# Two accumulator buffers of 1024 bytes, and a ring of weight buffers that starts 1856 bytes later

## The chip, the cores and the metric

The kernel runs on one core of one Trainium2 chip. The metric is device time in microseconds for one execution; a set of runs is told by its median, lowest and highest.

## The reference

Two transformer blocks run one after the other over 256 tokens of width 2048, in float32. What matters here is that nearly everything is a product of the 256 tokens with a large weight matrix, and that six plus three vectors of modulation come from a single row `c`:

```python
mod = (c_act @ w_ada[l] + b_ada[l])[:, None, :]
sh_a, sc_a, gt_a, sh_f, sc_f, gt_f = jnp.split(mod, N_ADA, axis=-1)
h = rms_norm(x, g_attn[l]) * (1.0 + sc_a) + sh_a
y = parallel_mixers(h, w_in[l], ...)                  # projections, two attentions, output products
x = x + gt_a * y
h = rms_norm(x, g_ffn[l]) * (1.0 + sc_f) + sh_f
x = x + gt_f * conv_ffn(h, w_up[l], w_conv[l], b_conv[l], w_down[l])
```

The second block has the same frame (three vectors from `w_mod`, a pool mixer with `pool_w_in`, `pool_w_grp` and `pool_w_out`), and a last norm.

## The kernel before, in words

**Weights.** Each weight matrix comes from memory in units of two K tiles by 512 columns, 512 KB each. `load_split` (lines 270 to 282) takes a buffer of the ring `raw` (`raw_tile`, line 118: six buffers of 4096 bytes on each partition), loads the unit into it from SyncE's queue, and splits it (lines 156 to 158) into a high part, which ScalarE casts, and a low part, which VectorE subtracts. Both parts lie in one buffer of the ring `hl` (line 279: five buffers of 8192 bytes). With `big=True` (lines 275 and 276) they lie instead in two buffers of the general pool `s4` (28 buffers of 4096 bytes, line 47). That is done for the last units of three products alone: three units at the end of `w_o` (line 992), three at the end of `w_down` (line 1098), five at the end of `pool_w_out` (line 1206).

**Products.** `gemm_gen` (line 366) makes a product in float32r with three passes (high by high, low by high, high by low). A unit gives 12 matmuls on line 378: for each of two token tiles and two K tiles, three of 512 columns. The stationary operand is a tile of activations, always in an `s4` buffer (`hT`, `hN`, `gThi`, `gTlo`, `pair`, `zT` and so on); the operand that streams through is the weight part `hl`. As a rule the six matmuls of one token tile are followed by the six of the other. With `tail` the last units make all matmuls of token tile 0 first and those of token tile 1 afterwards; with `head` the first three units do (lines 384 to 391).

**Modulation.** It is computed on VectorE while the products run. A vector unit (`vec_unit`, line 170) loads 512 KB of `w_ada` or `w_mod` into a buffer of the same ring `raw`, multiplies it with silu(c), which stands in two `s4` buffers, and leaves one sum for each partition in a column of the tile `vs`. `job_vec` (line 177) makes that tile (line 185) for a group of output tiles, adds its two halves at the end (line 189) and hands them on. There are 18 such tiles, all with the tag `vs`, which has two buffers. `pump` issues vector units between the units of a product, at a rate that each product names.

**Order.** Each engine's queue runs in program order. The first stage is scheduled by hand, the rest by the framework, which also places the buffers: a pool's tags in the order of their first use, one buffer behind the other, each as large as the largest tile that it holds.

**Places.** In the built program of before, the small constants come first. The `s4` buffers start at byte 34880 of a partition, 4096 bytes apart, so each starts 2112 bytes past a multiple of 4096. Behind them, at 149568, are the two `vs` buffers (96 bytes each), then the six of `raw` from 149760, the five of `hl` from 174336 and the four of `t2` from 215296. Every buffer of `raw` and `hl` starts 2304 bytes past a multiple of 4096.

Of the kernel before, what the change touches and what calls it, by code (L numbers as in the profile page):

```python
# [9 lines left out]
F32 = mybir.dt.float32  # L10
# [19 lines left out]
def block_pair_kernel(ctx: ExitStack, tc: tile.TileContext, T: dict, out: bass.AP):  # L30
# [54 lines left out]
    def load_c(name):  # L85
        """the row on one partition"""
        cr = [s4([128, 1024], name="crow") for _ in range(2)]
        for h in range(2):
            nc.sync.dma_start(cr[h][0:1, :], T[name][0:1, h * 1024:(h + 1) * 1024])
        return cr  # L90

    def bcast_c(cr, ps):
        """silu of the row, on every partition: [128, 2048], and the four steps that end it"""
        cb = [s4([128, 1024], name="cB") for _ in range(2)]
        acts = []

        def act(h, q, p):
            SC.activation(cb[h][:, q * 512:(q + 1) * 512], p, AF.Silu)
        for h in range(2):
            for q in range(2):  # L100
                p = ps([128, 512], name="cb")
                PE.matmul(p, lhsT=ones[0:1, :], rhs=cr[h][0:1, q * 512:(q + 1) * 512], start=True, stop=True)
                acts.append(lambda h=h, q=q, p=p: act(h, q, p))
                if ps is ps_at:
                    acts.pop()()
        return cb, acts

    def warm(dep, n):
        """products that nobody reads: they keep the array's clock up while it waits"""
        p = ps_at([128, 512], name="warm")  # L110
        for _ in range(n):
            PE.matmul(p[:, :128], lhsT=ones, rhs=dep, start=True, stop=True)

    def pump_to(n):
        """leaves n vector units waiting"""
        pump(max(0, len(jobs) - n))
# [53 lines left out]
    def vec_unit(W, ct, h, cv, acc):  # L170
        """acc <- the part of output tile ct of silu(c) @ W over the half h of K"""
        raw = raw_tile()
        nc.sync.dma_start(raw, T[W][ct, h])
        with tc.issue_after(gate[0]) if gate[0] is not None else nullcontext():
            V.scalar_tensor_tensor(raw, raw, 1.0, cact[cv][h], op0=OP.mult, op1=OP.mult, accum_out=acc)  # L175

    def job_vec(W, cv, cts, fin):
        """fin(columns) of silu(c) @ W for the output tiles cts"""
        n = len(cts)
        st = {}  # L180

        def unit(i, h):
            if i == 0 and h == 0:
                n_s4[0] += 1
                st["vs"] = sp.tile([128, 2, n], F32, name=f"vs_{n_s4[0]}", tag="vs", bufs=2)
            vs = st["vs"]
            vec_unit(W, cts[i], h, cv, vs[:, h, i:i + 1])
            if i == n - 1 and h == 1:
                tt(vs[:, 0], vs[:, 0], vs[:, 1], OP.add)
                fin(vs[:, 0])  # L190
        for i in range(n):
            for h in range(2):
                jobs.append(lambda i=i, h=h: unit(i, h))

    def job_row(W, cv, ct0, bcol, rows):
        """rows[h] = (silu(c) @ W + b)[ct0 * 128 + 1024 h ...] on every partition"""
        for h in range(2):
            def fin(v, h=h):
                tt(v, v, col(bcol + h * 8, 8), OP.add)
                rows[h] = s4([128, 1024], name="row")  # L200
                for q in range(2):
                    p = ps_at([128, 4, 128], name="rb")
                    for i in range(4):
                        j = q * 4 + i
                        PE.transpose(p[:, i, :], v[:, j:j + 1].to_broadcast([128, 128]), ident)
                    SC.copy(rows[h][:, q * 512:(q + 1) * 512], p.rearrange("p a b -> p (a b)"))
            job_vec(W, cv, range(ct0 + h * 8, ct0 + h * 8 + 8), fin)
# [26 lines left out]
    def norm_pair(o, j, sl, xT, rB, A, SH):  # L234
        """o <- split(xT * A * rB + SH) for K tiles 2j, 2j+1 and the tokens sl"""
        n = sl.stop - sl.start
        h = t2([128, 2, 256], name="hn")
        for i in range(2):
            k = 2 * j + i
            V.scalar_tensor_tensor(h[:, i, :n], xT[k // 4][:, k % 4, sl], A[:, k:k + 1], rB[:, sl], op0=OP.mult,  # L240
                                   op1=OP.mult)
            SC.activation(o[:, 0, i, sl], h[:, i, :n], AF.Identity, bias=SH[:, k:k + 1])  # L242
            r = V.scalar_tensor_tensor(o[:, 1, i, sl], h[:, i, :n], SH[:, k:k + 1], o[:, 0, i, sl], op0=OP.add,
                                       op1=OP.subtract)
# [7 lines left out]
    def h_prep(dst, src2, kk, A, SH):  # L252
        """dst <- split(src2 * A + SH) for K tiles kk, kk+1; src2 [128, 2, 256]"""
# [16 lines left out]
    def load_split(blk, n, big=False):  # L270
        """one unit: [128, KT * n], KT K tiles of n columns -> high and low parts [128, KT, n]"""
# [78 lines left out]
    def fill(n):  # L350
        """emits n units of the waiting products"""
        fcredit[0] += n
        while fcredit[0] >= 1.0 and fillers:
            try:
                next(fillers[0])
                fcredit[0] -= 1.0
            except StopIteration:
                fillers.popleft()

    def fill_to(gen):  # L360
        """emits the waiting products up to and with gen"""
# [4 lines left out]
    def gemm_gen(st, W, k0, nk, evac, rate=0.0, tail=0, head=0, kw=None, n=512, pre=(), ps=None,  # L366
                 part=(True, True)):
        """psum[t] = h[t] @ W over nk K tiles; W: units of KT K tiles; k0: first K tile of h, kw of W;
        part: whether this is the first, the last part of the sums in psum"""
# [38 lines left out]
    # the sums of these two chunks stay in psum  # L408
# [27 lines left out]
    for g in range(NG):  # L436
# [9 lines left out]
        if g == 0:  # L446
            # tables for the rotary embeddings
# [34 lines left out]
            def folded(o, n, f0, name):  # L482
                """tables with the gain folded in: g1 cos, g2 sin, g2 cos, g1 sin"""
# [8 lines left out]
    def rope(x1, x2, tabs, H, n):  # L492
        """x1, x2 [128, 2, H, n]; tabs: four [128, 2, n]"""
# [13 lines left out]
    # last K group: everything but the gates first  # L507
# [5 lines left out]
    def job_mod(W, cv, ct_sh, ct_sc, h, SH, A, bsh, bsc, gain):  # L513
        """the half h of SH and of A = (1 + scale) * gain"""
# [100 lines left out]
    # latent norms  # L615
# [7 lines left out]
    # sums of squares for qa, ka  # L623
# [47 lines left out]
    # k, q of attention A  # L671
# [36 lines left out]
    def softmax(ps, P, H, ns, scl):  # L708
        """P[:, h, :ns] = softmax of scl[h] * ps[:, h, :ns]"""
# [51 lines left out]
    def tanh_of(i):  # L761
        """sigmoid(g) = (1 + tanh(g / 2)) / 2; the last factor is in the split of the merged values"""
# [43 lines left out]
    for j in range(4):  # L806
# [3 lines left out]
        # keys: scale by their norm; rotary part shared by the heads  # L810
# [70 lines left out]
    def to_pairs(src, dst):  # L881
        """transposes four K tiles of src[:, t, :], halves and splits them, appends two pair tiles"""
# [31 lines left out]
    def residual_norm(c, t, p, rows, ss, xT):  # L914
        """the residual, its sum of squares and its transpose"""
# [9 lines left out]
    def pre_mean(ss, name):  # L925
        """the part of mean + eps that the first three chunks bring; also fetches the table of the root"""
# [7 lines left out]
    def rsqrt_last(ss, pre, t, name):  # L934
        """1/rms of the tokens of tile t, with one Newton step"""
# [10 lines left out]
    def norm_rows(ss, pre, name):  # L946
        """1/rms of each token, along the free axis of every partition, one token tile at a time"""
# [8 lines left out]
    def norm_pairs(o, js, sl, xT, rB, A, SH):  # L956
        """the same for the pairs js of one chunk, more of it on the scalar engine; overwrites xT"""
# [94 lines left out]
    # the first pairs in two halves of K, while the rest of the modulation arrives  # L1052
# [20 lines left out]
    def settle(c):  # L1073
        """the gated sum so far, onto x"""
# [171 lines left out]
def _layout(x):  # L1246
    """the inputs, rearranged (and repeated nowhere): no arithmetic, no change of type"""
    import numpy as np

    def blocks(w, n):  # L1250
        """[K, N] -> [N / n, K / 256, 128, 2 * n]: units of two K tiles by n columns"""
# [3 lines left out]
    def rows(w):  # L1255
        """[2048, N] -> [N / 128, 2, 128, 1024]: output features on the partitions"""
# [49 lines left out]
```

## Time and profile before

| | before |
|---|---|
| median of three runs | 1757.48 us (1755.73 to 1758.36) |
| the profiled execution: span from its first to its last instruction | 1753.6 us |
| TensorE matmul (PE) busy | 1719.4 us, 98% of the span, 7786 matmuls |
| TensorE weight load (PEld) busy | 1380.1 us, 79% |
| VectorE (DVE) busy | 1374.4 us, 78% |
| ScalarE (ACT) busy | 913.0 us, 52% |
| DMA queue of the weights | 454.19 MB, 77.0% of 16 engines' span |

The three times are of whole executions, the span is that of the one that was profiled; its own time is not listed apart from the three. Busy time of PE is the union of its matmuls' spans. Matmuls overlap in the pipeline, so that one that lasts about 0.39 us can follow the one before after much less. The distance from the start of one to the start of the next, here called the pitch, is what a stream of matmuls costs; it is read from the timeline: a run of n matmuls that lasts T, the last of them as long as the mean, has the pitch (T - mean) / (n - 1).

### The profile page before, as it was taken

The numbers are of one execution on the slowest core, as the hardware profiler recorded it, in microseconds if no ns is written. First come the engines' busy times: TensorE is split into PE (matmuls) and PEld (weight loads), VectorE is DVE, ScalarE is ACT, GpSimd is POOL, SyncE is SP. The second block draws the span as 40 slices with busy tenths as digits, with TensorE's granted clock in tenths as the row PEclk, the third lists the DMA queues.
The fourth block names the chain that finished last, engine by engine and source line by source line (L and its number), as shares of the span: only waits on it lengthen the run. The fifth ranks groups of instructions, "written<-read, shape, count | busy, mean of one in ns | idle before, by whom it ended". The sixth has DMA issues, their size and how long they took to land.

```text
span 1753.6 us, 22010 instructions
## 1 busy us (share of the span) xinstructions
PE 1719.4 (98%) x7786; PEld 1380.1 (79%) x7786; DVE 1374.4 (78%) x2079; ACT 913.0 (52%) x1283; POOL 4.2 (0%) x15
## 2 busy tenths in 40 slices
PE   8899999999999999999999999999999999999997
PEld 6688888878878878888887788777877777887886
DVE  8899899998978768589677676777877878765764
ACT  4644354767854456455455543555345574444443
POOL 0000000000000000000000000000000000000000
PEclk9999999999999999999999999999999999999999
DMA  8999988588879868677877777777877758778752
GB/s 326 338 327 317 330 309 286 192 285 292 284 225 319 285 206 315 213 240 228 297 243 247 232 253 273 251 252 266 269 259 258 252 167 267 261 241 269 237 190 90
DMA packets 127495, 455.59 MB, mean 260 GB/s; under 512 B 14357, under 2 KB 15893, under 8 KB 127385
## 3 DMA queue, kind: packets, MB, share of 16 engines
q1 hardware_dynamic: 127384, 454.19, 77.0%
q8 instruction: 61, 1.00, 0.2%
q14 instruction: 50, 0.40, 0.1%
HBM read 452.04 MB, written 2.10 MB: 259 GB/s over the span
## 4 chain that ended last, share of the span: by engine, by line
PE 88%; DVE 5%; DMA 4%; ACT 2%; issue 1%; ACTq 0%; SPq 0%; DVEq 0%
PE mm L378 79%; PE keep L378 2%; DVE hl L79 2%; DVE raw L175 1%; DMA raw<-in_w_mod 1%; PE tp L1025 1%; DMA raw<-in_w_ada 1%; PE mm L1171 1%; ACT hl L157 1%; PE dots L588 1%; DMA raw<-in_w_up 1%; DMA raw<-in_w_pb 0%; DVE xsq L79 0%; PE tp L1138 0%; DMA raw<-in_pool_w_in 0%
## 5 line engine op out<-in xcount | busy, mean ns | idle before, releaser
L157 ACT CAST hl<-raw 128x1024 fp32r<-128x1024 f32 (+2 forms) x564 | 588.2, 1046 | 639.6 <-PE mm L378 483.1
L79 DVE TENSOR_TENSOR hl<-raw,hl 128x1024 fp32r<-128x1024 f32 (+2 forms) x564 | 679.0, 1215 | 165.1 <-ACT hl L157 163.5
L378 PE MATMUL mm<-hl,hN 128*128 128x512 f32 x2880 | 689.0, 398 | 4.4 <-ACT hN L242 2.4
L378 PEld LDWEIGHTS mm<-hl,hN 128*128 128x128 f32 x2880 | 537.6, 188 | 134.5 <-DVE hN L79 3.4
L175 DVE SCALAR_TENSOR_TENSOR raw<-raw,cB 128x1024 f32<-128x1024 f32 x288 | 351.1, 1222 | 161.4 <-DMA raw<-in_w_mod 127.9
L378 PE MATMUL mm<-hl,hT 128*128 128x512 f32 (+1 forms) x1248 | 297.8, 397 | 7.3 <-ACT hl L157 3.2
L378 PEld LDWEIGHTS mm<-hl,hT 128*128 128x128 f32 x1248 | 234.6, 190 | 62.2 <-ACT hl L157 4.1
L378 PE MATMUL mm<-hl,gThi 128*128 128x512 f32 x704 | 221.1, 396 | 0.2
L378 PEld LDWEIGHTS mm<-hl,gThi 128*128 128x128 f32 x704 | 131.3, 187 | 32.8 <-DVE hl L79 0.8
L378 PE MATMUL mm<-hl,gTlo 128*128 128x512 f32 x352 | 138.2, 396 | 0.0
L378 PE MATMUL mm<-hl,pair 128*128 128x512 f32 x384 | 91.6, 395 | 0.0
L378 PE MATMUL mm<-hl,zT 128*128 128x512 f32 x384 | 89.6, 394 | 0.0
L378 PEld LDWEIGHTS mm<-hl,zT 128*128 128x128 f32 x384 | 71.7, 187 | 17.2
L378 PEld LDWEIGHTS mm<-hl,pair 128*128 128x128 f32 x384 | 71.3, 187 | 16.8
L378 PEld LDWEIGHTS mm<-hl,gTlo 128*128 128x128 f32 x352 | 66.0, 187 | 15.6
L79 DVE TENSOR_TENSOR pacc<-pacc,mm 128x512 f32<-128x512 f32 (+1 forms) x78 | 52.7, 676 | 11.4 <-PE mm L378 10.7
L1029 ACT ACTIVATE cv<-tp,wcv 128x256 f32<-128x256 f32 x88 | 44.9, 562 | 16.0 <-DVE cv L1033 8.5
L378 PE MATMUL mm<-hl,oaT 128*128 128x512 f32 x192 | 48.6, 403 | 0.0
L378 PE MATMUL mm<-hl,obT 128*128 128x512 f32 x192 | 48.0, 400 | 0.0
L378 PE MATMUL keep<-hl,hT 128*128 128x512 f32 x192 | 46.4, 397 | 1.0 <-DVE hl L79 1.0
L378 PEld LDWEIGHTS keep<-hl,hT 128*128 128x128 f32 x192 | 35.8, 188 | 10.1 <-DVE hl L79 2.1
L378 PEld LDWEIGHTS mm<-hl,obT 128*128 128x128 f32 x192 | 35.0, 188 | 8.3 <-DVE obT L79 0.4
(331 smaller groups left out, 1194.7 us busy)
## 6 DMA issues: line engine op xcount, KB each, us to landing
raw<-in_w_ada SPq DMA_DIRECT2D x192, 512.0 KB, 4.7
raw<-in_w_up SPq DMA_DIRECT2D x176, 512.0 KB, 4.6
raw<-in_w_in SPq DMA_DIRECT2D x112, 512.0 KB, 5.2
raw<-in_w_mod SPq DMA_DIRECT2D x96, 512.0 KB, 4.4
raw<-in_w_down SPq DMA_DIRECT2D x88, 512.0 KB, 4.6
raw<-in_pool_w_in SPq DMA_DIRECT2D x64, 512.0 KB, 4.4
raw<-in_w_o SPq DMA_DIRECT2D x32, 512.0 KB, 4.7
raw<-in_pool_w_out SPq DMA_DIRECT2D x32, 512.0 KB, 4.1
```

The lines of the kernel that those rows point to most:

```text
L79: return V.tensor_tensor(o, a, b, op=op)
L157: SC.copy(hi, src)
L175: V.scalar_tensor_tensor(raw, raw, 1.0, cact[cv][h], op0=OP.mult, op1=OP.mult, accum_out=acc)
L378: PE.matmul(ps[t][:, :n], lhsT=st(k0 + k, t, a), rhs=hl[b][:, i, :], start=(part[0] and k == 0 and x == 0), stop=(part[1] and k == nk - 1 ...
L588: PE.matmul(p[:, i, :], lhsT=qiT[h // 8][:, (h % 8) // 2, t * 128:(t + 1) * 128], rhs=kiT[:, h % 2, :ns], start=True, stop=True)
L1025: PE.transpose(p[:, i, t * 128:(t + 1) * 128], u[:, t, f * 128:(f + 1) * 128], ident)
L1029: SC.activation(cv[:, f, :], p[:, i, :], AF.Identity, bias=wcv[:, 3, fi:fi + 1], scale=wcv[:, 2, fi:fi + 1])
L1171: PE.matmul(pv[:, q, :], lhsT=hls[k // 2][wa][:, k % 2, f * 128:(f + 1) * 128], rhs=pooled[i][xb][:, k, :], start=(k == 0 and x == 0), sto ...
```

## The change

The two `vs` buffers get a fixed size of 2 by 128 float32 (1024 bytes) and each tile uses the first n columns of each half:

```diff
             if i == 0 and h == 0:
                 n_s4[0] += 1
-                st["vs"] = sp.tile([128, 2, n], F32, name=f"vs_{n_s4[0]}", tag="vs", bufs=2)
+                st["vs"] = sp.tile([128, 2, 128], F32, name=f"vs_{n_s4[0]}", tag="vs", bufs=2)[:, :, :n]
             vs = st["vs"]
```

The other lines of the diff take comments and docstrings out and leave empty lines in their place, so the line numbers stay. No instruction is added or taken away. Everything that the pool places behind `vs` moves: `raw`, `hl`, `t2` and the small buffers start 2 x 1024 - 2 x 96 = 1856 bytes later. `raw` then starts at 151616 and `hl` at 176192, 64 bytes past a multiple of 4096, with the same steps of 4096 and 8192 bytes as before. The constants and `s4` stay where they are.

## Rows read from the trace of the kernel before

**Rows 1.** The page: busy time of TensorE, and the chain by engine.
```profile
PE 1719.4 (98%) x7786; PEld 1380.1 (79%) x7786; DVE 1374.4 (78%) x2079; ACT 913.0 (52%) x1283; POOL 4.2 (0%) x15
...
PE 88%; DVE 5%; DMA 4%; ACT 2%; issue 1%; ACTq 0%; SPq 0%; DVEq 0%
```

**Rows 2.** Stretches, line 378's matmuls alone: start:end, length, busy (count), clock, DMA, GB/s.
```profile
31.00:96.00 65.00, 59.36 (x245) 0.97 0.92 327
96.00:270.00 174.00, 173.81 (x759) 1.00 0.91 322
270.00:521.00 251.00, 199.79 (x826) 1.00 0.77 260
521.00:613.00 92.00, 88.78 (x374) 1.00 0.87 295
613.00:657.00 44.00, 38.51 (x155) 0.96 0.64 211
657.00:1402.00 745.00, 727.65 (x3067) 1.00 0.77 256
1402.00:1486.00 84.00, 73.60 (x299) 0.98 0.66 214
1486.00:1622.00 136.00, 128.57 (x542) 1.00 0.79 258
1622.00:1720.00 98.00, 71.15 (x305) 1.00 0.65 210
1720.00:1753.60 33.60, 23.97 (x105) 0.92 0.18 63
```

**Rows 3.** Waits, whole span: who waited for whom, us, times, longest.
```profile
ACT hl L157 <- PE mm L378: 483.1, 313, 3.4
...
ACT hl L157 <- DMA raw<-in_w_in: 81.8, 48, 4.0
```

**Rows 4.** Waits, stretch 96 to 270 us.
```profile
ACT hl L157 <- DMA raw<-in_w_in: 70.0, 40, 4.0
ACT hl L157 <- PE mm L378: 18.3, 13, 2.4
```

**Rows 5.** Timeline of TensorE, weights in the ring `hl`: start, us, instruction, count.
```profile
96.31 63.86 PE L378 MATMUL mm<-hl,hT 128*128 128x512 f32 x273
...
1689.82 28.39 PE L378 MATMUL mm<-hl,zT 128*128 128x512 f32 x121
```

**Rows 6.** Timeline of TensorE, ends of `w_o` and `pool_w_out`, weights in `s4`.
```profile
640.46 5.83 PE L378 MATMUL mm<-hl,pair 128*128 128x512 f32 x25
...
1731.34 12.40 PE L378 MATMUL mm<-hl,zT 128*128 128x512 f32 x54
```

**Rows 7.** Timeline of TensorE, first three units of `pool_w_in` (`head`), weights in the ring.
```profile
1434.78 9.49 PE L378 MATMUL mm<-hl,hN 128*128 128x512 f32 x40
```

**Rows 8.** Timeline of the other engines beside the first of rows 6.
```profile
641.25 1.22 DVE L79 TENSOR_TENSOR hl<-raw,hl 128x1024 fp32r<-128x1024 f32 x1 [2.68 <-ACT hl L157]
...
643.15 1.05 ACT L157 CAST hl<-raw 128x1024 fp32r<-128x1024 f32 x1 [1.93 <-DMA raw<-in_w_up]
```

**Rows 9.** Groups of instructions by form: count, busy us, mean ns, idle before.
```profile
L79 DVE TENSOR_TENSOR hl<-raw,hl 128x1024 fp32r<-128x1024 f32 x548 | 663.7, 1222 | 162.1 <-ACT hl L157 160.6
L157 ACT CAST hl<-raw 128x1024 fp32r<-128x1024 f32 x548 | 575.0, 1052 | 630.9 <-PE mm L378 476.4 <-DMA raw<-in_w_in 81.8 <-issue 16.1
...
L79 DVE TENSOR_TENSOR cv<-cv,cv 128x1024 f32<-128x1024 f32 x11 | 13.4, 1222 | 0.0
...
L157 ACT CAST gThi<-cv 128x1024 fp32r<-128x1024 f32 x11 | 11.5, 1048 | 4.9 <-DVE A L79 2.6 <-DVE cv L79 2.3
```

**Rows 10.** Stretches of the whole core at the start; loads of `xT`, then `raw`.
```profile
1.80:8.20 6.40, 5.89 (x7) 2.49 (x8) 2.90 (x4) 2.52 (x5) 0.00 (x0) 1.00 0.89 326
8.60:13.00 4.40, 4.26 (x18) 3.40 (x16) 4.33 (x8) 2.83 (x3) 0.00 (x0) 1.00 1.04 420
13.00:31.00 18.00, 13.73 (x74) 13.05 (x74) 16.89 (x37) 5.24 (x9) 0.00 (x0) 0.91 0.94 352
```

## The prediction

> **What bounds the kernel now.** I read the page first, then the busy time by stretches, then the waits, and at last TensorE's timeline where the stretches say that it never stops. On the page TensorE's matmuls are busy for 98% of the span and make 88% of the chain that ended last [rows 1]. Busy matmuls overlap, so this says that the engine is never empty, not that it could go no faster. The waits confirm it from the other side: ScalarE, which makes the next weight part, waits 483.1 us in all for a matmul to free a buffer of the ring, and only 81.8 us for the loads of `w_in` [rows 3]. The producers stand behind TensorE in most of the kernel. By stretches, line 378's matmuls fill 727.65 of 745 us between 657 and 1402, which is the FFN, at a granted clock of 1.00 (the 2.4 GHz level) [rows 2]. From 96 to 270 us the rows show a second party: TensorE is as full as later, but ScalarE waits 70.0 us for loads and 18.3 us for TensorE [rows 4], and the DMA engines are 0.91 busy [rows 2]. There transfers are close to setting the pace too.
>
> So the question is what a matmul of line 378 costs in a stream, and whether an address can change that. With the weight part in the ring, 273 matmuls in 63.86 us and 121 in 28.39 us give a pitch of (63.86 - 0.39) / 272 = 0.2333 and (28.39 - 0.39) / 120 = 0.2333 us [rows 5]. The two runs are 1590 us apart and have different stationary operands and very different traffic beside them. The kernel also holds the same matmuls with the weight part elsewhere: in the `s4` buffers of `big=True`. There 25 matmuls take 5.83 us and 54 take 12.40 us: (5.83 - 0.39) / 24 = 0.2267 and (12.40 - 0.39) / 53 = 0.2266 us [rows 6]. Same shape, same types, stationary operand in `s4` both times; 6.7 ns less for each.
>
> Two other explanations are at hand, and the rows speak against both. The tail issues its matmuls in another order, all of one token tile first. The head of `pool_w_in` does that too, with weights in the ring: 40 matmuls in 9.49 us, (9.49 - 0.39) / 39 = 0.2333 us [rows 7]. Or the other engines are quiet at the end of the kernel. But the run at 640 us keeps 0.2267 us while VectorE and ScalarE split weights for the next product and a load has just landed [rows 8]. What is left is where the streamed operand lies.
>
> **The change part by part.**
>
> *The instructions.* None is added, removed or moved past another on a queue, SyncE's included. The sums in `vs` are single columns and the two adds over n columns read contiguous rows as before. I cost this at nothing, with no cover needed.
>
> *The place of `hl`.* It goes from 2304 to 64 bytes past a multiple of 4096. `s4` buffers start 2112 past it. A weight part is two K tiles of 2048 bytes, so in `s4` the streamed operand begins 2112 or 64 past a multiple of 4096. In the moved ring it begins 64 or 2112 past it: the same two places. In the old ring it was 2304 and 256. The stationary operands stay in `s4`, so their position against the streamed one is also that of the tails. I therefore take the tails' pitch for the whole kernel: 0.2333 - 0.2266 = 6.7 ns less per matmul. The bounds are 0 (place is not the cause) and 6.7 ns; a loss has no row that shows one, and I keep it for the rivals. I take 6.7 because both runs in `s4` give it to 0.1 ns.
>
> *What of it reaches the end.* Counts are from [rows 2], each times 6.7 ns, then the share that I expect to keep:
> - 657 to 1402: 3067, 20.5 us, all of it. ScalarE waits for TensorE here and the DMA share is 0.77; 3% more speed makes 0.79.
> - 1486 to 1622: 542, 3.6 us; 1622 to 1720: 305, 2.0 us; 521 to 613: 374, 2.5 us. All kept: DMA shares are 0.79, 0.65 and 0.87.
> - 1720 to the end: 105 less the 60 of the tail, which are fast already: 0.3 us.
> - 96 to 270: 759, 5.1 us. Transfers are near the pace, so I keep two thirds, 3.5 us.
> - 270 to 521, the attentions: 826, 5.5 us. Matmuls of line 378 cover 199.79 of 251 us and fill gaps of the short chains between; I keep half, 2.8 us.
> - 1402 to 1486: 299 less 36 of the tail, 1.8 us; norm chains set much of it, I keep 0.6.
> - 31 to 96: 245, 1.6 us, and 613 to 657: 155 less 36, 0.8 us. At the start VectorE and the loads set the pace, at the other the loads and the norm. I keep 0.3 and 0.
>
> Together 20.5 + 3.6 + 2.0 + 2.5 + 0.3 + 3.5 + 2.8 + 0.6 + 0.3 = 36.1 us. If everything were kept it would be 43.7 us; with the four stretches that TensorE clearly paces and the end, 28.9 us. Where the gain goes at the start, the next thing late is a load of `w_in` or `w_ada`.
>
> *The place of `raw`.* ScalarE and VectorE read it, the DMA engines write it. The two engines show no price for a place: VectorE's subtract takes 1222 ns from `raw` and `hl` and 1222 ns in `s4`, ScalarE's cast 1052 and 1048 ns [rows 9]. For the DMA engines the nearest row is the load of `xT`, whose `s4` buffers start 64 bytes past a multiple of 256, as the moved `raw` does; the old `raw` starts on one. Bandwidth over busy share is 326 / 0.89 = 366 GB/s for `xT`, and 420 / 1.04 = 404 and 352 / 0.94 = 374 GB/s for `raw` just behind [rows 10], 327 / 0.92 = 355 later [rows 2]. So loads may become up to 10% slower (404 against 366) or up to 3% faster (355 against 366). I take no change, since 366 lies between the values that `raw` itself shows.
>
> The Trainium skill's page "DMA: Bandwidth & Descriptors", section "How a descriptor splits into AXI transactions", speaks against this change: transactions start at multiples of 256 bytes, so a 4096-byte row at an offset of 64 takes 17 of them and, as an estimate, 130 beats in place of 128, 1.6% more. By that the DMA share between 96 and 270 us goes from 0.91 to 0.92 and the sum loses under 1 us; the rows are too coarse to tell 1.6%.
>
> **The sum.** The durations are of one execution with a span of 1753.6 us; its own whole time is not listed, and the median of the runs, 1757.5, is 3.9 us more, which the change doesn't touch. 1753.6 - 36.1 + 3.9 = 1721.4 us.
>
> **The rivals.**
>
> *No change.* The short pitch of the tails has a cause that I have not seen, or the ring does not land where I work out. For it: three tails are few, and no row shows an operand of the ring at another place. Against it: order and traffic are excluded by [rows 7, 8]. Time 1757.5. The Trainium skill's page "TensorE: Matmul & The Clock Gate", section "Back-to-back issue gap", gives a gap that depends on the columns alone (about 216 ns for 512, measured in isolation); by it no place could matter. The trace disagrees: two pitches for one shape, 0.2333 and 0.2266 us [rows 5, 6].
>
> *Gained and partly given back.* The pitch shrinks, but loads into the moved `raw` are the full 10% slower. Where they are 0.91 or 0.92 busy, 31 to 270 us, they would set the pace: busy share 0.92 x 1.10 / 0.94 = 1.077, with 0.94 taken as full [rows 10], so 239 x 0.077 = 18 us more, and from 521 to 613 0.87 x 1.10 / 0.94 = 1.018, 2 us. The gain there, 3.8 and 2.5 us, is gone. 1757.5 - 36.1 + 6.3 + 20 = 1748 us. The same band holds a pitch that shrinks by only part of 6.7 ns.
>
> *Slower.* The same 10%, and the pitch stays: 1757.5 + 20 = 1777 us. Transfers decide from the point at which a load takes 0.94 / 0.92, 2% more than now; below that they stay hidden. Against it: 366 GB/s for `xT` is no worse than 355 for `raw` later.
>
> **How the numbers follow.** A difference under about 0.2%, 3.5 us, can't be told from none. The forecast (pitch 0.2266, 28.9 to 43.7 us gained) gets 0.80, the partial case 0.09, no change 0.07, slower 0.04. Faster is the first two, 0.89. The forecast's own range is 1713.8 to 1728.6; with the runs' spread of 1.5 us and part of the second case it becomes 1712 to 1738.
>
> **What would show it.** Right: in the timeline of TensorE, runs of line 378 with weights in the ring have a pitch of 0.2266 us everywhere, the tails keep theirs, the FFN takes about 20 us less and ends about 30 us earlier, and the waits of ScalarE for TensorE shrink. Wrong: a pitch of 0.2333 with weights in the ring, or a DMA share over 0.95 with waits for loads that grow from 96 to 270 us.

## The result, and the profile after

| | before | after |
|---|---|---|
| median, in runs taken side by side | 1756.61 us (1753.21 to 1758.36, 4 runs) | 1742.39 us (1741.28 to 1744.28, 4 runs) |
| the profiled execution | span 1753.6 us | 1743.09 us, span 1741.3 us |

The ratio of after to before is 0.9911, with a 95% interval from 0.9887 to 0.9935. The change gains about 14 us. The forecast was 36.1 us, at 1721.4, and the time lies outside its range of 1712 to 1738.

The first thing to look at is the pitch, in TensorE's timeline (start, us, instruction, count): a stretch of the first projections, one of the FFN, one of the pool mixer and one of the last product, all with weights in the ring.

```profile
95.90 64.31 PE L378 MATMUL mm<-hl,hT 128*128 128x512 f32 x283
1087.66 21.57 PE L378 MATMUL mm<-hl,hN 128*128 128x512 f32 x94
...
1483.04 19.91 PE L378 MATMUL mm<-hl,hN 128*128 128x512 f32 x87
...
1645.19 67.06 PE L378 MATMUL mm<-hl,zT 128*128 128x512 f32 x295
```

(64.31 - 0.39) / 282 = 0.2267 us, and in the same way 0.2277, 0.2270 and 0.2268. (The second run holds a short break, which the merging of the timeline covers.) The ring now has the pitch of [rows 6], where it had 0.2333 us in [rows 5]. So the pitch fell as forecast. The next view asks what came of it: line 378's matmuls by stretches, as in [rows 2].

```profile
96.00:270.00 174.00, 173.18 (x776) 144.59 (x775) 1.00 0.92 329
...
657.00:1402.00 745.00, 716.86 (x3075) 576.12 (x3074) 0.99 0.77 256
```

From 96 to 270 us, 776 matmuls fit where 759 did. In the 745 us that were the FFN's before it is 3075 in place of 3067, and TensorE is busy for 716.86 us with them in place of 727.65. A stream that takes 3% less each brought next to nothing here: TensorE now has breaks. The page says where the chain went (busy time of the engines; chain by engine, then by line; two groups with count, busy us, mean ns and the idle time ahead of them).

```profile
PE 1692.9 (97%) x7786; PEld 1385.5 (80%) x7786; DVE 1369.1 (79%) x2079; ACT 910.8 (52%) x1283; POOL 4.2 (0%) x15
...
PE 59%; DMA 18%; DVE 14%; issue 5%; ACT 3%; SPq 0%; DVEq 0%; ACTq 0%
PE mm L378 51%; DMA raw<-in_w_mod 13%; DVE hl L79 5%; DMA raw<-in_w_ada 4%; DVE raw L175 3%; PE keep L378 2%; ACT hl L157 1%; PE mm L1171 1%; DVE cv L1031 1%; PE tp L1025 1%; DVE score L599 1%; DVE cv L1033 0%; DVE pacc L79 0%; PE tp L922 0%; DMA cst<-in_cst 0%
...
L175 DVE SCALAR_TENSOR_TENSOR raw<-raw,cB 128x1024 f32<-128x1024 f32 x288 | 350.5, 1220 | 184.7 <-DMA raw<-in_w_mod 139.9
...
L1029 ACT ACTIVATE cv<-tp,wcv 128x256 f32<-128x256 f32 x88 | 44.9, 562 | 47.9 <-DVE cv L1033 39.4
```

TensorE's part of the chain fell from 88% [rows 1] to 59%; loads of `w_mod` have 13% and VectorE 14%. The waits of the whole span (who waited for whom: us, times, longest):

```profile
ACT hl L157 <- PE mm L378: 432.0, 284, 4.4
...
DVE raw L175 <- DMA raw<-in_w_mod: 139.9, 73, 5.3
```

ScalarE waits 51 us less for TensorE than in [rows 3].

Both kernels issue the same instructions in the same order on every engine, so the two traces can be laid side by side by TensorE's weight loads, in their order. The table has, for each stretch of before, the gain that the forecast counted in full, what it kept, and how much shorter the stretch between the same two weight loads is after (the two last columns are from versions that come later: a_again is the changed kernel itself in another execution, a_spare moves some of VectorE's work):

```
stretch of before   in full   kept   after   a_again   a_spare
0 to 96               1.6      0.3    0.2     1.1       1.5
96 to 270             5.1      3.5    4.7     4.7       4.7
270 to 521            5.5      2.8    0.3    -0.7       0.7
521 to 613            2.5      2.5    1.7     0.3       1.7
613 to 657            0.8      0     -0.3    -0.6       0.3
657 to 1402 (FFN)    20.5     20.5    0.6     9.0      15.7
1402 to 1486          1.8      0.6   -0.4     0.7       1.5
1486 to 1622          3.6      3.6    2.9     2.9       2.9
1622 to 1720          2.0      2.0    2.2     1.9       2.0
1720 to the end       0.3      0.3    0.3     0.3       0.3
sum                  43.7     36.1   12.2    19.6      31.3
```

One row holds 19.9 of the 23.9 us that are missing: the FFN. Inside it the gain comes through from 1010 to 1200 (5.0 us) and from 1245 to 1360 (3.0), but from 1200 to 1245 and from 1360 to 1402, the ends of the third and fourth round, the kernel takes 5.0 and 5.5 us longer than before; against the full gain that is 13 us. The other 7 are missing ahead of 1010 us. The profiled execution, 1743.09 us, is one of the slower ones of this kernel, a_spare's (1723.98) the fastest of five. In a_again (1735.7 us) the FFN gives 9.0 us, and the same two places take 1.8 and 2.3 us longer than before. The windows of 4 us at the first of these, in the profiled execution (busy of PE, PEld, DVE, ACT, POOL with counts; granted clock, DMA share, GB/s):

```profile
1208.00:1212.00 4.00, 4.00 (x20) 3.30 (x19) 3.54 (x8) 2.00 (x4) 0.00 (x0) 1.00 0.92 294
1212.00:1216.00 4.00, 2.37 (x11) 1.64 (x9) 4.00 (x9) 0.94 (x2) 0.00 (x0) 1.00 0.74 226
1216.00:1220.00 4.00, 2.93 (x8) 2.30 (x9) 4.00 (x4) 1.97 (x2) 0.00 (x0) 0.72 0.73 244
1220.00:1224.00 4.00, 4.00 (x16) 3.25 (x15) 2.08 (x4) 1.05 (x1) 0.00 (x0) 0.85 0.80 260
1224.00:1228.00 4.00, 4.00 (x19) 3.30 (x19) 4.00 (x6) 1.87 (x2) 0.00 (x0) 1.00 0.76 259
```

TensorE stops for 2.7 us while VectorE is busy without a break, and behind the stop the granted clock is 0.72 and 0.85: part of the time it is at 1.2 GHz, which costs, by an estimate from these windows, another (0.28 + 0.15) x 4 = 1.7 us. The same stop in a_again lasts 2.0 us, and the clock stays at 1.00:

```profile
1212.00:1216.00 4.00, 1.99 (x9) 1.35 (x8) 4.00 (x5) 2.00 (x2) 0.00 (x0) 1.00 0.66 220
1216.00:1220.00 4.00, 3.60 (x17) 2.64 (x16) 3.08 (x4) 1.00 (x1) 0.00 (x0) 1.00 0.90 274
```

What TensorE waited for is in the timeline, first of after:

```profile
1205.29 1.22 DVE L175 SCALAR_TENSOR_TENSOR raw<-raw,cB 128x1024 f32<-128x1024 f32 x1 [3.01 <-DMA raw<-in_w_mod]
...
1213.98 0.39 PE L378 MATMUL mm<-hl,gTlo 128*128 128x512 f32 x1
1214.67 1.22 DVE L79 TENSOR_TENSOR cv<-cv,cv 128x1024 f32<-128x1024 f32 x1
...
1215.97 1.05 ACT L157 CAST gThi<-cv 128x1024 fp32r<-128x1024 f32 x1 [3.06 <-DVE cv L79]
...
1217.07 2.35 PE L378 MATMUL mm<-hl,gThi 128*128 128x512 f32 x6 [2.70 <-ACT gThi L157]
```

and the same of before, with the weight load ahead of the matmul (`gThi` is a stationary operand):

```profile
1215.76 1.22 DVE L175 SCALAR_TENSOR_TENSOR raw<-raw,cB 128x1024 f32<-128x1024 f32 x1 [3.01 <-DMA raw<-in_w_mod]
...
1226.41 1.05 ACT L157 CAST gThi<-cv 128x1024 fp32r<-128x1024 f32 x1
...
1227.78 1.35 PEld L378 LDWEIGHTS mm<-hl,gThi 128*128 128x128 f32 x6
...
1228.01 1.56 PE L378 MATMUL mm<-hl,gThi 128*128 128x512 f32 x6
```

`w_down` needs the gate of the round's last pair, which VectorE finishes (`cv`) and ScalarE casts (`gThi`). Before, the cast ended at 1227.46; the weight load began at 1227.78 and the matmul at 1228.01: 0.55 us to spare for the matmul, 0.32 for its weight load. After, the cast begins 10.4 us earlier than before, but TensorE is through with its last matmul at 1213.98 + 0.39 = 1214.4, 13.6 us ahead of its 1228.01. VectorE had not kept up. Ahead of this point it stands for 3.01 us in front of a load of `w_mod`, with its convolutions queued behind. That wait is not new: before has one of 3.01 us at the same instruction, and from this instruction to the cast pass 10.65 us before and 10.68 after. VectorE's part did not get shorter, and its small cover was gone.

At the end of the fourth round the stop is longer, and there TensorE waits for a split (`hl`), which stands in VectorE's queue behind the same kind of work:

```profile
1377.85 0.52 PE L378 MATMUL mm<-hl,gThi 128*128 128x512 f32 x1 [3.37 <-DVE hl L79]
```

How VectorE had stood could be seen in the profile of before, in views that the prediction did not use. The stretch 1010 to 1200 of the kernel before, all engines, and its waits:

```profile
1010.00:1200.00 190.00, 190.00 (x833) 151.87 (x832) 138.36 (x184) 89.54 (x104) 0.00 (x0) 1.00 0.78 259
```

```profile
ACT hl L157 <- PE mm L378: 78.9, 49, 2.4
DVE raw L175 <- DMA raw<-in_w_mod: 43.2, 22, 3.6
DVE hl L79 <- ACT hl L157: 7.6, 12, 1.6
```

VectorE is busy for 138.36 us, 73%, and waits 43.2 us for loads of `w_mod` and 7.6 us for ScalarE. An engine that works in order is always busy or waiting, so that the sum, 189.2 of 190, says nothing by itself; what counts is for whom it waits. The wait for ScalarE can shrink with the pitch, because ScalarE waits for TensorE here (78.9 us). The wait for loads need not, and it did not. The same work of after, and VectorE's waits there:

```profile
1000.50:1185.50 185.00, 185.00 (x833) 152.03 (x832) 135.07 (x180) 87.28 (x101) 0.00 (x0) 1.00 0.79 259
```

```profile
DVE raw L175 <- DMA raw<-in_w_mod: 44.8, 23, 4.2
DVE hl L79 <- ACT hl L157: 5.8, 8, 1.5
```

The work takes 5.0 us less, and the wait for loads is as long as before. Work and loads together fill 181.6 of 190 us before and 179.9 of 185 after. This stretch still gave its gain; that it used up VectorE's distance ahead of TensorE, which is missing at the end of the round, fits these rows.

### The profile page after: what moved, and what is told of

Read it like the earlier page. It is cut to its first block, busy times and chain, and to the rows that moved or that the text cites. A ratio compares the mean times of both kernels' runs of the same rounds, so it can differ in the third digit from the quotient of the medians.

```text
span 1741.3 us, 22010 instructions
## 1 busy us (share of the span) xinstructions
PE 1692.9 (97%) x7786; PEld 1385.5 (80%) x7786; DVE 1369.1 (79%) x2079; ACT 910.8 (52%) x1283; POOL 4.2 (0%) x15
## 4 chain that ended last, share of the span: by engine, by line
PE 59%; DMA 18%; DVE 14%; issue 5%; ACT 3%; SPq 0%; DVEq 0%; ACTq 0%
PE mm L378 51%; DMA raw<-in_w_mod 13%; DVE hl L79 5%; DMA raw<-in_w_ada 4%; DVE raw L175 3%; PE keep L378 2%; ACT hl L157 1%; PE mm L1171 1%; DVE cv L1031 1%; PE tp L1025 1%; DVE score L599 1%; DVE cv L1033 0%; DVE pacc L79 0%; PE tp L922 0%; DMA cst<-in_cst 0%
## 5 line engine op out<-in xcount | busy, mean ns | idle before, releaser
L157 ACT CAST hl<-raw 128x1024 fp32r<-128x1024 f32 (+2 forms) x564 | 586.6, 1046 | 584.5 <-PE mm L378 432.0
L378 PE MATMUL mm<-hl,hN 128*128 128x512 f32 x2880 | 676.4, 394 | 6.6 <-DVE hN L79 2.4
L175 DVE SCALAR_TENSOR_TENSOR raw<-raw,cB 128x1024 f32<-128x1024 f32 x288 | 350.5, 1220 | 184.7 <-DMA raw<-in_w_mod 139.9
L378 PE MATMUL mm<-hl,hT 128*128 128x512 f32 (+1 forms) x1248 | 290.9, 392 | 8.0 <-ACT hT L157 3.3
```

The lines of the kernel that those rows point to most:

```text
L157: SC.copy(hi, src)
L378: PE.matmul(ps[t][:, :n], lhsT=st(k0 + k, t, a), rhs=hl[b][:, i, :], start=(part[0] and k == 0 and x == 0), stop=(part[1] and k == nk - 1 ...
```

## The experiments: what makes the pitch

The expectations name theories by letters; each says what its letters mean.

**a_shift** puts 192 bytes among the constants, ahead of all rings, so that the ring `hl` returns to the places that it had before (256 past a multiple of 4096), while `s4` moves with it and keeps its distance to the ring. It was run once.

```diff
+    pad = const([128, 48], name="pad")
+    GP.memset(pad, 0.0)
```

> The kernel after with 192 bytes of padding ahead of all pools: s4 (stationary operands) and hl (streamed operands) both move by 192, to multiples of 256, so their places against each other stay as in the kernel after. Theory P (the place of the two operands against each other makes the pitch): 0.2267 us, about 1742 us. Theory Q (the streamed operand's own place makes it): 0.2333 us, as with the old ring, and about 1757 us.

Measured: 1734.99 us, and this row of the timeline: (64.31 - 0.39) / 282 = 0.2267 us.

```profile
95.93 64.31 PE L380 MATMUL mm<-hl,hT 128*128 128x512 f32 x283
```

The ring stands where it stood in the slow kernel, and the pitch is short. So the distance between the streamed and the stationary operand decides, not the place of the streamed one. The time was 5 to 7 us under that of the changed kernel, with `raw` on a multiple of 256 in this version, so that question got two sets of runs, **a_shift2** (the same kernel) and **a_again** (the changed kernel).

> The kernel after with 192 bytes of padding ahead of all pools, timed in rounds: hl keeps its place against s4 and so its pitch of 0.2267 us, and raw goes back to a multiple of 256. Theory D (a load into raw at 64 past a multiple of 256 takes longer, as between 8.5 and 13 us of the kernel after, and VectorE, which waits for these loads, hands it on): 1734 to 1738 us, 5 to 8 us under the kernel after. Theory E (the one look at 1735.0 us was the spread of runs): within 3 us of the kernel after.

> The kernel after, unchanged, on the same chip as the next two, as their base: 1742 us (1739 to 1745).

Measured: a_shift2 1741.0 us, ratio 0.9891 (0.9872 to 0.991); a_again 1740.27 us, ratio 0.9888 (0.987 to 0.9906). No difference, so theory E holds: the single execution had been at the low end of a spread. After's own runs here go from 1735.7 to 1741.84.

**b_hl64** and **b_hl128** take the kernel before and put 64 or 128 bytes between `raw` and `hl`, so that `raw` stays where it was and the ring alone moves. It then starts 256 or 320 bytes past the place of an `s4` buffer, modulo 2048, where before has 192.

```diff
+        gap = sp.tile([128, 16], F32, name="gap", tag="gap", bufs=1)
+        GP.memset(gap, 0.0)
```

(32 elements in b_hl128.)

> The kernel before with an unused buffer of 64 bytes between raw and hl: raw stays exactly where it was before, hl moves by 64, to 256 bytes past the places of s4 modulo 2048 (the kernel after has it at 0 past, the kernel before at 192). If 0 and 256 past count alike (the pattern repeats every 256 bytes), the pitch is 0.2267 us, and by theory D the time is that of the run above, 1734 to 1738 us; by theory E 1739 to 1745 us. If the pattern repeats only every 512 bytes or more, the pitch is another one.

> The kernel before with an unused buffer of 128 bytes between raw and hl: hl stands 64 bytes past the places of s4 modulo 256. Theory P (the place of the two operands against each other makes the pitch) says that it differs from 0.2333 us, without saying which way; if only 0 past is fast it is between 0.2267 and 0.2400 us. Time 1735 to 1790 us.

Measured: b_hl64 1734.95 us, ratio 0.9869 (0.9847 to 0.9892); b_hl128, run once, 1740.76. Their rows of the timeline, b_hl64 first:

```profile
95.75 64.53 PE L380 MATMUL mm<-hl,hT 128*128 128x512 f32 x284
...
1659.75 40.51 PE L380 MATMUL mm<-hl,zT 128*128 128x512 f32 x178
```

```profile
95.56 64.71 PE L380 MATMUL mm<-hl,hT 128*128 128x512 f32 x282
...
1659.62 40.77 PE L380 MATMUL mm<-hl,zT 128*128 128x512 f32 x174
```

In b_hl64 the pitch is (64.53 - 0.39) / 283 = 0.2266 and (40.51 - 0.39) / 177 = 0.2267 us; in b_hl128 it is 0.2289 with `hT` and 0.2334 with `zT`. A distance of 0 or 256 gives the short pitch, 192 the long one, 320 (64 modulo 256) one between the two or the long one, by operand. That fits a pattern that repeats every 256 bytes; other distances were not run. It also shows that the move of the ring alone makes the gain, without the move of `raw`. The median of b_hl64 lies where theory D had it, but a_shift2, whose `raw` also starts on a multiple of 256, is at the time of a_again, and the intervals of all three overlap; the last section of experiments comes back to `raw`.

## The experiments: where the rest of the gain went

**a_noload** and **b_noload** leave out the loads and products of `w_mod` in the kernels after and before: VectorE does an operation of the same size on the resident vector (1218 ns in place of 1220). There are 96 such units; the first expectation's 64 is a miscount.

```diff
+        if W == "w_mod":
+            with tc.issue_after(gate[0]) if gate[0] is not None else nullcontext():
+                V.scalar_tensor_tensor(cact[cv][h], cact[cv][h], 1.0, cact[cv][h], op0=OP.mult, op1=OP.max, accum_out=acc)
+            return
         raw = raw_tile()
```

> The kernel after, but the 64 vector units of w_mod load nothing: they run the same instruction on silu(c) in place, so the shift and scale of the second block's modulation and its gate are not those of the reference. Theory A (VectorE runs in order and stands at each vector unit until its load has landed; with the shorter pitch it can no longer keep its lead, and TensorE stalls at the ends of the FFN rounds): without the loads the lead holds, the stalls of 5 us near 1203 and 1366 us go, and the kernel takes 1725 us or less, 28 us (24 to 32) less than the same edit of the kernel before. Theory B (the arithmetic that VectorE and ScalarE do at the end of a round is too long for the shorter pitch, loads or not): the stalls stay and the difference to the same edit of the kernel before stays near 15 us.

> The kernel before with the same edit: the vector units of w_mod load nothing, so that part of the modulation is left out. TensorE's pitch of 0.2333 us paces it from 657 to 1402 us with or without these loads, so theories A and B both expect about the time of the kernel before, 1750 to 1757 us; it is the base for the run above.

Measured: a_noload 1721.72 us, ratio 0.9795 (0.9778 to 0.9812); b_noload 1751.66 us, ratio 0.9967 (0.9956 to 0.9978). Without these loads the offset is worth 29.9 us, as theory A had it, and theory B falls. The loads cost 5.5 us before the change and 19 to 21 after it. But this takes away a wait and 50 MB of traffic at once.

**a_nowait** parts the two: the same insertion, but behind the load, which is still made into the ring `raw`.

```diff
         raw = raw_tile()
         nc.sync.dma_start(raw, T[W][ct, h])
+        if W == "w_mod":
...
+            return
```

> The changed kernel, in which the 96 loads of w_mod are still made, in the same ring of six buffers, but VectorE does not read them: it does an operation of the same size on the resident vector instead, and so never waits for them. (Left out: the products with w_mod; its sums are wrong numbers.) It separates the two readings of the run without these loads (1721.7 us). Theory A (VectorE, in its order behind a load that has not landed, is what holds the weight stream): the waits of L175 for w_mod are gone, the time falls to between 1719 and 1726 us. Theory F (the loads themselves fill the DMA engines, and what the run without them gained it gained from 48 MB less to move): the splits wait for their own weights instead, the time stays between 1735 and 1742 us. In between: both, in the share that it shows.

Measured: 1722.31 us (1719.72 to 1723.65), ratio 0.9789 (0.9762 to 0.9816), as without the loads. Its chain:

```profile
PE 82%; DVE 9%; DMA 5%; issue 2%; ACT 2%; SPq 0%; ACTq 0%; DVEq 0%
```

The bytes cost nothing that can be measured, and theory F falls. What costs is that VectorE, which works in order, stands in front of them with splits and convolutions behind it. In the trace the ends of the third and fourth round are 0.9 and 0.7 us shorter than before, where after takes 5.0 and 5.5 longer. Some 6 us more than in after come behind the FFN, from 1402 to 1486 and from 1622 to 1720, and there b_noload too is 3.2 and 2.0 us shorter than before: that part comes without the short pitch, too. (This version also frees a load buffer as soon as its load has landed, and does not part that from the wait; a_spare below leaves it as it was and mends the same two places.)

Two versions tried to take the wait away by queueing. **a_lag** issues the product of a vector unit behind the next unit's split, so that its load has more time.

```diff
+            flush()
+            late_use.append(done)
-            vec_unit(W, cts[i], h, cv, vs[:, h, i:i + 1])
```

> The kernel after, but from the FFN rounds on each vector unit's VectorE instruction is issued one weight unit later than its load, so that it stands behind the next subtraction in VectorE's queue. The same bytes are loaded. Theory A: VectorE waits less for w_mod (139.9 us now, under 90 then) and the kernel gains 6 to 14 us on the kernel after: 1728 to 1736 us. Theory C (the loads are late because the DMA engines have no more to give, whoever waits): no gain, 1739 to 1746 us, the waits only move to ScalarE.

Measured: 1739.95 us, ratio 0.9903 (0.9887 to 0.992), the time of theory C. But its reason isn't seen either: the wait did not move at all, to ScalarE or elsewhere.

```profile
DVE raw L188 <- DMA raw<-in_w_mod: 139.8, 71, 3.9
```

**a_raw8** gives `raw` eight buffers and `hl` four.

```diff
-    NS4, NRAW, NHL = 28, 6, 5
+    NS4, NRAW, NHL = 28, 8, 4
```

> The changed kernel with eight buffers for loads instead of six, and four pairs of split weights instead of five (the same memory, all offsets kept modulo 4096). Theory R (a load starts only when VectorE has freed the buffer of six units before, so its landing time of 4.5 us shows up as a wait): with eight it starts two units, some 3.5 us, earlier; VectorE's wait for w_mod falls from 140 to under 70 us and the time to 1722 to 1732 us, unless the fifth pair was needed. Theory F (the DMA engines are full in these stretches): the waits and the time stay within 4 us. Theory H (the fifth pair of split weights is what carries TensorE through): slower than the changed kernel, 1745 us or more, with waits of TensorE for the splits.

Measured: 1745.05 us (1738.11 to 1748.69), ratio 0.9915 (0.9886 to 0.9944). The wait fell, by less than theory R wanted, the time is at the bound of theory H (though TensorE's waits for the splits are 9.9 us, as in after), and ScalarE's wait for a pair of split weights rose from 432.0 to 536.2 us:

```profile
ACT hl L157 <- PE mm L378: 536.2, 352, 4.0
DVE raw L175 <- DMA raw<-in_w_mod: 113.8, 72, 3.8
```

So neither more distance nor more load buffers, at the price of a pair of split weights, helps. What paces the loads of `w_mod` in detail stays open; longer rings of both kinds at once were not tried.

## The experiments: which waits have to go

**a_rates** and **b_rates** move vector units from the up projections to the down projections.

```diff
-    FR, FD = 0.45, 0.4
+    FR, FD = 0.3, 0.64
```

> The changed kernel with the vector units of the modulation moved from the up projections (0.45 to 0.30 of one per weight unit) to the down projections (0.40 to 0.64), the same number in all. In the up projections VectorE also has the convolutions to do. Theory A (in these stretches VectorE, its own work plus its waits for loads, is the pace once TensorE's pitch is 0.2267 us): VectorE keeps its distance to TensorE through the up projections, the stalls of TensorE at the ends of the rounds shrink, and the time falls by 5 to 12 us, to 1729 to 1736 us. Theory F (the bytes are the limit, whenever they come): no change within 4 us. Slower, if 1.64 loads per weight unit in the down projections are more than the DMA engines bring (316 GB/s would be wanted): 1745 us or more.

> The kernel before with the same move of the vector units (0.45 to 0.30 and 0.40 to 0.64). There the pitch is 0.2333 us and TensorE is busy without a break from 657 to 1402 us. Theory A: TensorE is the bound there and VectorE has cushion, so the move is worth nothing: within 3 us of the kernel before. If the move gains as much here as in the changed kernel, then VectorE was no new bound of the change, and theory A falls.

Measured: a_rates 1729.98 us, ratio 0.9841 (0.9813 to 0.9869); b_rates 1753.84 us, ratio 0.9978 (0.996 to 0.9997). Counted from the kernel before in the same set of runs, that is 28.8 us where the change alone gains 14.2 and 18.9 (a_again): 10 to 15 us on the changed kernel. On the kernel before it is 4 to 5, a little more than the 3 that theory A allowed. In the trace of a_rates the end of the third round is nearly mended (0.4 us longer than before), that of the fourth is not (6.1 us longer).

**a_spare** moves only the 12.6 units that fall into the last half pairs of the four rounds. **a_spare2** does that and lowers the rate elsewhere too (0.40 and 0.61). **b_spare2** is a_spare2 with the offset of b_hl64.

```diff
-    FR, FD = 0.45, 0.4
+    FR, FD = 0.45, 0.55
...
-    def ffn_pair(j, rate):
+    def ffn_pair(j, rate, rate1):
...
-        up_half(j, 1, k, nk, rate)
+        up_half(j, 1, k, nk, rate1)
...
-            ffn_pair(j, FR)
+            ffn_pair(j, FR, FR if j < j1 - 1 else 0.0)
```

> The changed kernel with no vector unit in the last half pair of each round of the FFN (28 weight units, 12.6 vector units), and these units spread over the down projections instead (0.40 to 0.55 of one per weight unit); the rate elsewhere in the up projections stays 0.45. Theory A1 (what stalls TensorE is the place: VectorE, late behind loads of w_mod just where it has the last convolution and gate of a round to do, with TensorE waiting for their result): the stalls at the ends of the third and fourth round, 10.5 us together, go below 4 us, and the time falls to 1729 to 1735 us, as much as with the lower rate everywhere (1730.0 us). Theory A2 (VectorE loses its distance all through the up projections, at 0.45 units per weight unit): it arrives late at the last half pair all the same, the time falls by less than 5 us, to 1736 to 1741 us.

> The same with 0.40 in the rest of the up projections and 0.61 in the down projections. Theory A1: no better than with 0.45 and 0.55, within 3 us of it. Theory A2: 4 us or more below it. If both count, it is the fastest version of the changed kernel so far, 1724 to 1729 us; slower than 1733 us would say that the loads in the down projections (1.61 per weight unit) have become the limit.

> The kernel before with the gap of 64 bytes ahead of the ring of split weights (the load buffers stay where the kernel before has them) and the rates of the run a_spare2. Theory G (the load buffers of the changed kernel, 64 bytes past a multiple of 256, cost some 2% per load and with it part of the gain): 3 us or more below a_spare2. Theory A alone: within 3 us of it.

Measured: a_spare 1727.29 us (1723.98 to 1729.8), ratio 0.983 (0.9809 to 0.985); a_spare2 1732.59 us, ratio 0.9851 (0.9831 to 0.9872); b_spare2 1730.3 us, ratio 0.9847 (0.9826 to 0.9868). In a_spare the ends of the third and fourth round look like this:

```profile
1190.00:1230.00 40.00, 40.00 (x180) 32.68 (x179) 32.98 (x42) 19.32 (x22) 0.00 (x0) 1.00 0.84 279
1330.00:1380.00 50.00, 50.00 (x230) 40.16 (x229) 41.23 (x58) 28.30 (x39) 0.00 (x0) 1.00 0.76 251
```

TensorE does not stop and the clock stays at 1.00. VectorE still waits for `w_mod`, only not ahead of the gate:

```profile
DVE raw L175 <- DMA raw<-in_w_mod: 116.2, 69, 4.1
```

Most of the wait remained (116.2 of 139.9 us) and most of the time came back: the place of the wait decides, as theory A1 had it, not its sum. The two round ends are now 1.0 and 0.6 us shorter than before, as in a_nowait, which kept VectorE's work there and took away the wait. Theory A2 falls: a lower rate elsewhere brought nothing more. a_spare2 is even 5 us slower than a_spare, more than the 3 us that theory A1 allowed; no run tells why.

The last two complete a table of kernels with and without either edit: **b_spare** is the kernel before with a_spare's move, **b_hl64_spare** the same with the 64-byte gap.

> The kernel before (no offset changed, pitch 0.2333 us) with the vector units moved as in a_spare (none in the last half pair of a round, 0.55 in the down projections). Theory A1 (the wait at the end of a round became TensorE's only because the pitch fell): here TensorE has no stall there, so the move is worth little by itself, 0 to 5 us, 1753 to 1758 us; what the offset brings on top of it (1727.3 us with both) is then 26 to 31 us, against 16 to 18 us without it. If it brings 10 us or more alone, the move is a gain of its own and has nothing to do with where the gain of the change was lost.

> The kernel before with the gap of 64 bytes ahead of the ring of split weights and the vector units of a_spare. Theory G (the load buffers 64 bytes past a multiple of 256 cost part of the gain): 1719 to 1724 us, below a_spare's 1727.3. Without it: within 3 us of a_spare.

Measured: b_spare 1757.63 us, ratio 0.9996 (0.9982 to 1.001); b_hl64_spare 1727.45 us, ratio 0.9828 (0.9811 to 0.9845).

(medians, each of its own set of runs)

```
                                     rates as before   a_spare's move
ring 192 bytes off (before)              1757.5           1757.6
ring on a multiple of 256 (after)        1742.4           1727.3
the same, `raw` not moved                1735.0           1727.5
```

The move of the vector units is worth nothing by itself. Counted from the kernel before in the same set of runs, the change alone gains 14.2 us here and 18.9 in a_again, with the move 30.9: the move is worth 12 to 17 us with the change. With the ring alone moved it is worth 6 us (24.2 and 30.4). And with the move the place of `raw` costs nothing that these runs can tell: theory G falls.

## Why the prediction was wrong, step by step

**Pitch: right, to 0.1 ns.** The tails of [rows 6] gave the right value, and the two places in the ring behave alike. The reason that I gave for taking it was sound as well: position against the stationary operand. The rival "no change" is refuted: for 512 columns the pitch is 0.2333, 0.2289 or 0.2267 us by place alone. The Trainium skill's page "TensorE: Matmul & The Clock Gate", section "Back-to-back issue gap", makes the gap of isolated matmuls depend on the columns alone; this kernel's stream does not follow that.

**Instructions at no cost: right.** The order on every engine is the same.

**`raw` at no cost: right for the time.** The mean 4096-byte packet from 8.5 to 13 us took 162.6 ns after and 160.0 before, 1.6% more, which agrees in size with the estimate from the Trainium skill's page "DMA: Bandwidth & Descriptors", section "How a descriptor splits into AXI transactions", though the page tells it of reads and here it is the written side that moved. With `raw` on a multiple of 256 again it is 159.3 ns (a_shift2) and 159.7 (b_hl64). From 96 to 270 us nothing of it is seen: the mean packet took 183.9 ns before and 181.6 after. The share went from 0.91 to 0.92 there, the number that was worked out, but by luck: more was moved in the same time (329 GB/s for 322). ScalarE's wait for `w_in` there is 68.3 us against the 70.0 of [rows 4].

**"657 to 1402: 3067, 20.5 us, all of it. ScalarE waits for TensorE here and the DMA share is 0.77": the step that failed.** 0.6 us came in the profiled execution and 9.0 in a_again. I read ScalarE's wait as the slack of all producers, and the DMA share as the slack of the loads. VectorE was left out of the sum: its waits for `w_mod` (43.2 us from 1010 to 1200) were not free time, since the work behind them could not pass. At the ends of the rounds TensorE needs a result of VectorE, and at the third 0.55 us of cover was there; TensorE came 13.6 us earlier, the cast behind VectorE 10.4. With the waits gone (a_nowait) or moved to another place (a_spare), these places give their gain, and 15.7 of the 20.5 us come in a_spare. The clock, which the sum left at 1.00, had a part too: by an estimate from the granted clock, the FFN of the profiled execution lost some 7 us to the 1.2 GHz level, 2.1 at its start, 1.7 at 968 us (0.58 from 968 to 972) and 1.7 behind each of the two stops; before and a_spare lost none in their FFN, a_again 1.7. The range failed with the same step: its lower gain, 28.9 us, took this stretch as sure.

**The other stretches.** 96 to 270 gave 4.7 us for 3.5 kept, so loads were further from the bound than I took them to be. 0 to 96 gave 0.2 for 0.3, but 1.1 in a_again. 270 to 521 gave 0.3 for 2.8: the matmuls that fill gaps in the attentions gave next to nothing back; that the short chains there set the time fits, but no run tests it. 521 to 613 and 1486 to 1622 lost some 0.7 us each, 1402 to 1486 gave -0.4 for 0.6. Differences of 1 us between executions of the changed kernel are common in the table, so little hangs on these.

**The rivals.** "Gained and partly given back" came nearest in time (1748) and named the wrong cause: transfers up to 10% slower. No rival had VectorE as the next bound.

**What stays open.** The first 130 us of the FFN are 0.3 us shorter after and 0.0 in a_nowait, but 2.6 in a_spare, 2.8 in a_again and 3.5 in a_rates. Most of this goes with the granted clock. The FFN begins at 650.4 us in after, at 648.1 in a_spare and at 652.2 in a_again; the first two windows below are of after, then one of a_spare and one of a_again:

```profile
648.00:652.00 4.00, 3.42 (x9) 2.25 (x8) 3.44 (x10) 2.72 (x9) 0.00 (x0) 0.50 0.23 56
652.00:656.00 4.00, 4.00 (x14) 3.16 (x13) 4.00 (x10) 3.49 (x10) 0.00 (x0) 0.68 0.37 124
...
648.00:652.00 4.00, 3.89 (x17) 3.25 (x18) 4.00 (x12) 3.02 (x9) 0.00 (x0) 1.00 0.41 131
...
652.00:656.00 4.00, 3.83 (x17) 3.18 (x18) 4.00 (x12) 3.02 (x9) 0.00 (x0) 1.00 0.38 131
```

Why after begins its FFN at the lower level and a_again, the same kernel, does not, no run tells; and a_spare2 gives 0.3 us there without it. Ahead of 1010 us the FFN gave 2.9 us in after, 5.0 in a_again and 6.2 in a_spare of some 9.7, and 1.7 in a_nowait: what is missing there is not the wait for `w_mod`, and beyond the clock its cause stays open. And a_spare is still 5.9 us above the 1721.4 of the forecast.

## What to carry to other kernels

Before a gain on the busiest engine is counted in full, ask of each other engine that works in order, stretch by stretch, for whom it waits. Waits for the fast engine shrink when that one gets faster; waits for loads, with work queued behind, need not (43.2 and 44.8 us here, for an engine that is 73% busy). Then look at the few points where the fast engine needs a result of that engine, and read the time to spare there (here 0.55 us); work that can be done at any time is kept away from them. A gain in one place may need a second edit, worth nothing by itself, before it shows.

## What was not expected of the hardware

- A float32r matmul of 512 columns in a stream takes 0.2267 us or 0.2333 us, by the distance in bytes between its streamed and its stationary operand in a partition: 0 or 256 past each other (modulo 2048) the short one, 192 the long one, and at 320 it is 0.2289 or 0.2334 by operand. Moving both operands together by 192 bytes did not matter (a_shift).
- A stop of TensorE of 2.7 us was followed by two windows of 4 us at a granted clock of 0.72 and 0.85, so that by an estimate it cost 1.7 us more than its own length. In another execution of the same kernel a stop of 2.0 us at the same place left the clock at 1.00.
